# Two-layer encoder trunk: residual and output products kept token by feature, x turned between the layers

## The chip, the cores and the metric

One NeuronCore of one Trainium2 chip runs the whole program in one launch. The metric is the device time of that launch in microseconds, as a median of timed executions. Shapes: 256 tokens, 2048 features, float32 in and out. SBUF and PSUM have 128 partitions, so 256 tokens are two blocks of 128 and 2048 features are sixteen.

## What is computed

Layer 0 has one input projection that feeds attention heads (A) and a gated MLP (B); both halves, side by side, go through one output projection. Layer 1 is a recurrent block with its own input and output projections. Each layer starts with an RMS norm and ends with a residual add, and a last RMS norm closes the program. Cut to what the change touches:

```python
def rms_norm(x, g):
    y = x * lax.rsqrt(jnp.mean(x * x, axis=-1, keepdims=True) + NORM_EPS)
    return y * g

# layer 0: y_a and y_b are (256, 2048) each
x = x + jnp.concatenate([y_a, y_b], axis=-1) @ ab_w_out[0]     # (4096, 2048)
# layer 1: h * silu(z_c) is (256, 2688)
xn = rms_norm(x, c_norm[0])
proj = xn @ c_w_in[0]                                          # (2048, 5376)
...
x = x + (h * jax.nn.silu(z_c)) @ c_w_out[0]                    # (2688, 2048)
return rms_norm(x, final_norm)
```

## The kernel before

Every product is made in three parts from float32 split into a high and a low piece, both of type fp32r: high by high, high by low and low by high. The weights stream from HBM in *chunks*: usually 16 tiles of 128 by 128, as two *units* of 8 tiles (512 KB). For each unit SyncE issues the load into `raw` (L202), ScalarE copies it to `hi` (L220) and VectorE subtracts to get `lo` (L234). `raw`, `hi` and `lo` are rings of 6 buffers, so the splits run up to three chunks ahead of TensorE and the loads up to three more.

`run(emit)` (L268) writes out one chunk: work that was put down with `at(step, fn, phase)` (L253) is called in phases around the two splits and the chunk's matmuls. Phase -1 comes before the splits, 0 to 1.5 between the splits and the matmuls, 2 behind the matmuls. Each engine then runs its own instructions in the order in which they were written; this order is fixed by hand, with no scheduler.

There are two ways to emit a chunk:

- `feat` (L300), *feature by token*: a weight tile is the stationary operand and the activations move. For each tile one matmul of 512 columns takes `hi` against both pieces of x (256 tokens each, L312), and one of 256 columns takes `lo` against the high piece (L316). The output is a block of 128 features by 256 tokens, in two halves that must be added. With `whole=True`, used for the last block of an output product, three matmuls of 256 columns go to one half (L307 to L309).
- `tokn` (L320), *token by feature*: 128 tokens of the activations are stationary and 512 weight columns move. For each row of 128 by 512 weights (four tiles) and each token block three matmuls of 512 columns run (L328 to L330), so 24 for a chunk of 16 tiles. The output is 128 tokens by 512 features, with nothing to add up afterwards. Before the change `tokn` serves v, z_a (`ps_v`, `ps_za`) and the values of B (`ps_vb`).

All three output products go through `feat`: `ob` (the B half of layer 0, `do_ob`, 16 chunks), `oa` (the A half, 16 chunks) and `co` (layer 1, 21 chunks). The residual `res` lies feature by token from the start, since x comes in transposed as `xT`. A finished block is added in two steps (`res_add`, L384).

Between the layers, `x1_add` (L753) forms x's high pieces for layer 1 from the block (times `c_norm`), squares it on ScalarE (L373), and GpSimd adds the squares up in `acc` (L380); `x1_lo` makes the low piece. `norm_at` then sums `acc` over partitions by matmuls with ones (L350), takes the power -0.5 on GpSimd (L356) and spreads it over partitions by matmuls with the identity (L361) into `rb`.

At the end `x2_add` does the same for the last norm and multiplies with `final_norm` on ScalarE (L962). After the last block the sums are formed (L350), raised to -0.5 (L356), spread (L361), and VectorE scales all of `res` in nine pieces, each stored by a DMA from SyncE or ScalarE (L971, L972).

Of the kernel before, what the change touches and what calls it, by code (L numbers as in the profile page):

```python
# [37 lines left out]
for _n, _w in (("g0", KD), ("hn", KD), ("lng", KD), ("lnb", KD), ("g1", KD), ("gf", KD),  # L38
               ("cw0", KC), ("cw1", KC), ("cw2", KC), ("cw3", KC), ("cb", KC),
               ("ba", KC), ("bx", KC), ("lam", KC), ("ident", P)):  # L40
    PRM[_n] = (_at, _w)
    _at += _w
NPRM = _at

# [24 lines left out]
def plan():  # L69
# [23 lines left out]
    def out(kind, rows, wait):  # L93

        cols, late = wait
        order = [(f, k) for f in range(cols) for k in range(late)]
        order += [(f, k) for f in range(cols) for k in range(late, rows)]
        order += [(f, k) for f in range(cols, KD) for k in range(rows)]
        for t in range(0, len(order), 16):
            add(kind, fk=order[t:t + 16], n=len(order[t:t + 16]))  # L100

    heads(0)
    for f in range(KD):
        add("ob", f=f, n=16)
# [4 lines left out]
    out("oa", KD, (4, KD - 4))  # L109
    for j in range(LEAD):  # L110
        add("xb", j=j, n=16)
    for j in range(KC):
        if j + LEAD < KC:
            add("xb", j=j + LEAD, n=16)
# [4 lines left out]
    out("co", KC, (4, KD))  # L119
# [8 lines left out]
def trunk(ctx, tc, xT, prm, rep, wsp, wst, out):  # L128
# [30 lines left out]
    res = cpool.tile([P, KD, S], F32, name="res")  # L159
# [36 lines left out]
    def load(u):  # L196
# [7 lines left out]
        for q in range(a // 4, b // 4):  # L204
            if c == 0 or q == 0 and c < 4:
                ks = slice(q, q + 1) if c == 0 else slice(4 * c, 4 * c + 4)
                SP.dma_start(res[:, ks, :], xT[:, ks, :])
            s = slice((q * 4 - a) * P, (q * 4 - a + 4) * P)
            SP.dma_start(t[:, s], src[:, s])

    def split_x(k):
        A.activation(x.hi[k], res[:, k, :], AF.Copy, scale=par("g0", k))
        V.scalar_tensor_tensor(x.lo[k], res[:, k, :], par("g0", k), x.hi[k].bitcast(F32),
                               op0=ALU.mult, op1=ALU.subtract)
# [105 lines left out]
    def tokn(pss, hi, lo, kq, first, last):  # L320

        for k in range(4):
            s = slice(k * 512, (k + 1) * 512)
            a, b = first and k == 0, last and k == 3
            for t in range(NT):
                xs = slice(t * P, (t + 1) * P)
                xk, xm = x.hi[4 * kq + k][:, xs], x.lo[4 * kq + k][:, xs]
                T.matmul(pss[t], xk, hi[:, s], start=a, stop=False)  # L328
                T.matmul(pss[t], xk, lo[:, s], start=False, stop=False)  # L329
                T.matmul(pss[t], xm, hi[:, s], start=False, stop=b)  # L330
# [13 lines left out]
    def r_sum(more=()):  # L344

        ps = pst.tile([P, 512], F32, tag="t", name="ps_r")
        srcs = [acc, *more]
        for t in range(NT):
            for n, a in enumerate(srcs):
                T.matmul(ps[:, t:t + 1], a[:, t * P:(t + 1) * P], ones[:, 0:1],  # L350
                         start=n == 0, stop=n == len(srcs) - 1)
        return ps

    def r_pow(ps):
        V.tensor_scalar(rt, ps[:, 0:NT], 1.0 / DM, EPS, op0=ALU.mult, op1=ALU.add)
        GP.tensor_tensor(rt, rt, mhalf, op=ALU.pow)  # L356
# [7 lines left out]
    def norm_at(s):  # L364

        box = []
        at(s, lambda: box.append(r_sum()), 2)
        at(s + 1, lambda: r_pow(box[0]))
        at(s + 1, lambda: A.copy(rb, r_spread()[:, :S]), 2)

    def squares(f):
        sq = spool.tile([P, S], F32, tag="sqr", name="sqr")
        A.activation(sq, res[:, f, :], AF.Square)  # L373
        return sq

    def add_squares(f, sq):
        if f == 0:
            GP.tensor_scalar(acc, sq, 1.0, 0.0, op0=ALU.mult, op1=ALU.add)
        else:
            GP.tensor_tensor(acc, acc, sq, op=ALU.add)  # L380

    def res_add(f, ps, whole=False):
        for a in (0, S)[:1 if whole else 2]:
            V.tensor_tensor(res[:, f, :], res[:, f, :], ps[:, a:a + S], op=ALU.add)  # L384
# [10 lines left out]
    def token_chunks(name):  # L395

        pss = [mm_tile(f"ps_{name}_{t}") for t in range(NT)]
        for kq in range(4):
            run(lambda hi, lo: tokn(pss, hi, lo, kq, kq == 0, kq == 3))
        return pss  # L400

# [38 lines left out]
    with tc.tile_pool(name="pb", bufs=2) as pb:  # L440
# [11 lines left out]
        def x_squares(q):  # L452
            A.activation(sq[:, q * 1024:(q + 1) * 1024],
                         res[:, 4 * q:4 * q + 4, :].rearrange("p k s -> p (k s)"), AF.Square)
# [11 lines left out]
        norm_at(5)  # L466
# [142 lines left out]
    with tc.tile_pool(name="pa", bufs=2) as pa:  # L609
# [125 lines left out]
        def do_ob(f):  # L735
            def emit(hi, lo):
                ps = mm_tile(f"ps_ob{f}")
                feat(ps, hi, lo, ALL, y, True, True)
                at(pos[0] + 1, lambda: res_add(f, ps))
            run(emit)  # L740

# [3 lines left out]
        for f in range(KD):  # L745
            do_ob(f)
# [6 lines left out]
        def x1_add(f, ps):  # L753
            res_add(f, ps, f == KD - 1)
            A.activation(x.hi[f], res[:, f, :], AF.Copy, scale=par("g1", f))
            add_squares(f, squares(f))

        def x1_lo(f):
            V.scalar_tensor_tensor(x.lo[f], res[:, f, :], par("g1", f), x.hi[f].bitcast(F32),
                                   op0=ALU.mult, op1=ALU.subtract)  # L760

        def out_product(kind, rows, done):

            cur = {}
            while pos[0] < len(chunks) and chunks[pos[0]]["kind"] == kind:
                def emit(hi, lo):
                    fk = chunks[pos[0]]["fk"]
                    for f in dict.fromkeys(f for f, _ in fk):
                        tiles = [(w, k) for w, (g, k) in enumerate(fk) if g == f]
                        k0, k1 = tiles[0][1], tiles[-1][1]  # L770
                        if k0 == 0:
                            cur[f] = mm_tile(f"ps_{kind}{f}")
                        feat(cur[f], hi, lo, tiles, y, k0 == 0, k1 == rows - 1, f == KD - 1)
                        if k1 == rows - 1:
                            done(f, cur.pop(f), pos[0])
                run(emit)

        def x1_done(f, ps, s):
            if f == KD - 1:
                at(s, lambda: x1_add(f, ps), 2)  # L780
                at(s, lambda: x1_lo(f), 2)
            else:
                at(s + 1, lambda: x1_add(f, ps))
                at(s + 1, lambda: x1_lo(f), 1)
# [5 lines left out]
    with tc.tile_pool(name="pc", bufs=2) as pc:  # L790
# [102 lines left out]
        norm_at(s0)  # L893

        def do_xb(j):
            def emit(hi, lo):
                ps = mm_tile(f"ps_xb{j}")
                feat(ps, hi, lo, ALL, x, True, True)
                s = max(pos[0] + 1, s0 + 2 + (j > 1))
                at(s, lambda: xb_scale(j, ps), -1)  # L900
                at(s, lambda: xb_tap(j), 0.5)
                at(s, lambda: xb_conv(j), 1)
                at(s + 1, lambda: xb_hi(j), 0.5)
                at(s + 1, lambda: xb_lo(j), 1)
            run(emit)

# [34 lines left out]
        for j in range(LEAD):  # L941
            do_xb(j)
        for j in range(KC):
            at(pos[0], lambda j=j: seam(j), 1)
            if j + LEAD < KC:
                do_xb(j + LEAD)
# [6 lines left out]
        last = []  # L953

        def x2_add(f, ps):
            res_add(f, ps, f == KD - 1)
            sq = squares(f)
            if f < KD - 1:
                add_squares(f, sq)
            else:  # L960
                last.append(sq)
            A.activation(res[:, f, :], res[:, f, :], AF.Copy, scale=par("gf", f))  # L962

        out_product("co", KC, lambda f, ps, s: at(min(s + 1, len(chunks) - 1), lambda: x2_add(f, ps),
                                                  2 if s == len(chunks) - 1 else 0))
        r_pow(r_sum(last))
        rbp = r_spread()[:, :S]
        f = 0
        for q, w in enumerate((1, 1, 2, 2, 2, 2, 2, 2, 2)):
            fs = slice(f, f + w)  # L970
            V.tensor_tensor(res[:, fs, :], res[:, fs, :], rbp.unsqueeze(1).broadcast_to([P, w, S]), op=ALU.mult)  # L971
            (SP, A)[q % 2].dma_start(out[:, fs, :], res[:, fs, :])  # L972
            f += w


def pack(np, i):
# [9 lines left out]
    for c in chunks:  # L986
# [12 lines left out]
        elif kind == "ob":  # L999
            src = rows(wo0, KD, KD, P * c["f"], P)  # L1000
        elif kind in ("xb", "zc"):
            src = rows(w1, 0, KD, (kind == "zc") * CW + P * c["j"], P)
        elif kind in ("oa", "co"):
            src = np.concatenate([rows(wo0 if kind == "oa" else wo1, k, 1, P * f, P) for f, k in c["fk"]], axis=1)
# [26 lines left out]
    put("gf", i["final_norm"])  # L1031
# [9 lines left out]
    rep = np.concatenate([i["ab_sgu_b"][0].reshape(-1), i["ab_lambda"][0].reshape(-1)])  # L1041
# [22 lines left out]
```

## Time and profile before

| | us |
|---|---|
| median of 3 runs (lowest to highest) | 1248.69 (1248.47 to 1249.19) |
| the profiled execution's own time | 1249.09 |
| its span, first to last instruction | 1247.3 |
| TensorE matmul busy | 1234.3 (99%) |
| VectorE busy | 868.0 (70%) |
| ScalarE busy | 680.6 (55%) |
| GpSimd busy | 62.8 (5%) |
| HBM traffic over the span | 185 GB/s |

The span is the profiled execution's time less 1.79 us outside the first and last instruction. Busy times are shares of the span. A matmul's printed duration overlaps the next one's, so rates of TensorE are read from the distance of starts, not from durations. The chain of waits follows what ended last back to the start.

### The profile page before, as it was taken

The page shows a single profiled execution, that of the slowest core. Times are in us where ns is not written, and L with a number is a line of the kernel's source. Part 1 is how long each engine was busy: PE and PEld are TensorE (multiplying, and loading weights), DVE is VectorE, ACT ScalarE, POOL GpSimd, SP SyncE. Part 2 cuts the span into 40 slices and gives each one's busy share as a digit, 9 for nine tenths or more (in the row PEclk, how much of TensorE's full clock was granted, in tenths as well). Part 3 has the DMA queues.
Part 4 walks back from the last instruction along what each step waited for, and adds up shares of the span by engine and source line. Part 5 has one row for each costly group of instructions (what it writes and reads, how often), then busy time and mean ns, then how long its engine had stood idle before and what let it go on. Part 6 is the DMA issues. An engine that isn't in the chain of part 4 may idle for free.

```text
span 1247.3 us, 18370 instructions
## 1 busy us (share of the span) xinstructions
PE 1234.3 (99%) x6903; PEld 1080.2 (87%) x6903; DVE 868.0 (70%) x1359; ACT 680.6 (55%) x1093; POOL 62.8 (5%) x96
## 2 busy tenths in 40 slices
PE   9999999999999999999999999999999999999996
PEld 7888888888888888888888888888889889988885
DVE  6847777776566646646746746767899999988553
ACT  7544454444454344544444545545788887886541
POOL 1100000000000000000000000110000000001111
PEclk9999999999999999999999999999999999999998
DMA  9854555555645654555555555564655666657541
GB/s 331 283 181 168 184 184 182 184 179 190 204 148 182 199 194 167 189 180 169 186 174 173 183 178 171 189 199 154 198 196 201 220 194 201 199 179 237 190 135 68
DMA packets 69400, 234.57 MB, mean 188 GB/s; under 512 B 8000, under 2 KB 8896, under 8 KB 69312
## 3 DMA queue, kind: packets, MB, share of 16 engines
q1 hardware_dynamic: 66240, 227.84, 54.8%
q0 software_dynamic: 1920, 3.15, 1.0%
q10 hardware_dynamic: 1152, 2.42, 0.6%
q8 instruction: 54, 0.88, 0.3%
q14 instruction: 34, 0.28, 0.1%
HBM read 228.13 MB, written 2.10 MB: 185 GB/s over the span
## 4 chain that ended last, share of the span: by engine, by line
PE 97%; issue 1%; DVE 1%; DMA 1%; SPq 0%; ACT 0%; POOLq 0%; POOL 0%; DVEq 0%; ACTq 0%
PE ps_xb L312 6%; PE ps_zc L312 6%; PE ps_co L312 6%; PE ps_zb L312 5%; PE ps_k L312 5%; PE ps_ob L312 5%; PE ps_q L312 5%; PE ps_u L312 5%; PE ps_oa L312 4%; PE ps_zc L316 3%; PE ps_xb L316 3%; PE ps_co L316 3%; PE ps_k L316 2%; PE ps_ob L316 2%; PE ps_u L316 2%; PE ps_q L316 2%
## 5 line engine op out<-in xcount | busy, mean ns | idle before, releaser
L234 DVE TENSOR_TENSOR lo<-raw,hi 128x1024 fp32r<-128x1024 f32 (+2 forms) x423 | 503.4, 1205 | 185.4 <-ACT hi L220 180.2
L220 ACT CAST hi<-raw 128x1024 fp32r<-128x1024 f32 (+2 forms) x423 | 427.2, 1037 | 246.4 <-PE ps_za L330 50.0
L312 PE MATMUL ps_xb<-x,hi 128*128 128x512 f32 x336 | 83.8, 392 | 0.0
L312 PE MATMUL ps_zc<-x,hi 128*128 128x512 f32 x336 | 83.6, 391 | 0.0
L312 PE MATMUL ps_co<-y,hi 128*128 128x512 f32 x315 | 77.8, 391 | 0.0
L312 PEld LDWEIGHTS ps_zc<-x,hi 128*128 128x128 f32 x336 | 61.8, 188 | 11.8
L312 PEld LDWEIGHTS ps_xb<-x,hi 128*128 128x128 f32 x336 | 61.8, 188 | 11.2
L312 PEld LDWEIGHTS ps_co<-y,hi 128*128 128x128 f32 x315 | 56.9, 189 | 10.3
L312 PE MATMUL ps_zb<-x,hi 128*128 128x512 f32 x256 | 65.0, 396 | 0.0
L312 PE MATMUL ps_q<-x,hi 128*128 128x512 f32 x256 | 63.7, 393 | 0.0
L312 PE MATMUL ps_u<-x,hi 128*128 128x512 f32 x256 | 63.7, 391 | 0.0
L312 PE MATMUL ps_k<-x,hi 128*128 128x512 f32 x256 | 63.4, 393 | 0.0
L312 PE MATMUL ps_ob<-y,hi 128*128 128x512 f32 x256 | 62.8, 394 | 0.0
L312 PE MATMUL ps_oa<-y,hi 128*128 128x512 f32 x240 | 59.0, 392 | 0.5 <-DVE res L384 0.5
L312 PEld LDWEIGHTS ps_u<-x,hi 128*128 128x128 f32 x256 | 47.0, 188 | 9.1
L312 PEld LDWEIGHTS ps_q<-x,hi 128*128 128x128 f32 x256 | 47.1, 188 | 9.0
L312 PEld LDWEIGHTS ps_ob<-y,hi 128*128 128x128 f32 x256 | 47.1, 188 | 9.0
L312 PEld LDWEIGHTS ps_k<-x,hi 128*128 128x128 f32 x256 | 47.1, 188 | 8.9
L312 PEld LDWEIGHTS ps_zb<-x,hi 128*128 128x128 f32 x256 | 47.1, 189 | 8.5
L312 PEld LDWEIGHTS ps_oa<-y,hi 128*128 128x128 f32 x240 | 43.7, 188 | 8.9 <-PE ps_oa L312 0.9
L328 PE MATMUL ps_vb<-hi,x 128*128 128x512 f32 x128 | 51.1, 399 | 0.2 <-ACT hi L226 0.2
L329 PE MATMUL ps_vb<-lo,x 128*128 128x512 f32 x128 | 50.3, 393 | 0.7 <-DVE lo L227 0.7
(296 smaller groups left out, 2302.5 us busy)
## 6 DMA issues: line engine op xcount, KB each, us to landing
raw<-in_wst SPq DMA_DIRECT2D x402, 512.0 KB, 3.9
raw<-in_wst SPq DMA_DIRECT2D x30, 256.0 KB, 6.0
raw<-in_wst SPq DMA_DIRECT2D x15, 384.0 KB, 3.3
seam<-xcp POOLq DMA_DIRECT2D x9, 192.0 KB, 3.1
res<-in_xT SPq DMA_DIRECT2D x3, 512.0 KB, 6.9
out_x<-res SPq DMA_DIRECT2D x4, 256.0 KB, 2.3
seam<-xcp POOLq DMA_DIRECT2D x6, 128.0 KB, 2.3
out_x<-res ACTq DMA_DIRECT2D x3, 256.0 KB, 2.4
```

The source lines that it names most:

```text
L220: A.copy(hi[:, :(b - a) * P], raw[u][:, :(b - a) * P])
L234: V.tensor_sub(lo[:, :n], raw[u][:, :n], hi[:, :n].bitcast(F32))
L312: wide = lambda i: T.matmul(ps, hi[:, col(tiles[i][0])], m.both[tiles[i][1]], start=first and i == 0, stop=last and i == n - 1)
L316: T.matmul(ps[:, :S], lo[:, col(w)], m.hi[k], start=False, stop=False)
L328: T.matmul(pss[t], xk, hi[:, s], start=a, stop=False)
L329: T.matmul(pss[t], xk, lo[:, s], start=False, stop=False)
```

## The change

The residual `res` becomes token by feature: 128 tokens by 2048 features for each of two token blocks. It takes the room of the feature-major copy of x, which only the first chunks read; a second copy of x, `xt`, 2 MB in token layout, is loaded into that room at step 24 by two DMAs of ScalarE's queue.

The three output products use `tokn`, in four column blocks `cb` of 512 features. A chunk is four rows of 128 by 512 weights; in `co` (21 rows) the last chunk of a column block has five, so `co` has 20 chunks instead of 21. The residual add is one 512-column step for each token block. The squares are summed along the features by ScalarE's accumulating output (`ssq`), so GpSimd's additions and the matmuls with ones go in layer 1 and at the end.

Layer 1 still wants x feature by token. So after each column block of `oa`, eight TensorE transposes (`x1_turn`) bring it to PSUM, and ScalarE and VectorE make the high and low pieces from there (`x1_parts`). To leave time for the last column block, the first two chunks of `xb` take rows 0 to 11 of the first two feature blocks first and rows 12 to 15 last (`early`).

At the end `final_norm`, copied over 128 partitions, is loaded at step `s1 + 8` by eight DMAs of ScalarE's queue (1 MB) and multiplied in for column blocks 0 to 2 by VectorE while `co` runs (`gf_mult`). The last chunk does the first token block's matmuls, then the second's (`apart`); each token block is then normed, scaled and stored by itself (`finish`), with all eight stores on SyncE.

```diff
-    def out(kind, rows, wait):
-        cols, late = wait
-        order = [(f, k) for f in range(cols) for k in range(late)]
...
+    def out(kind, rows):
+
+        for cb in range(4):
+            for k in range(0, rows - 3, 4):
+                nk = rows - k if rows - k < 8 else 4
+                add(kind, cb=cb, k0=k, nk=nk, n=4 * nk)
...
+    early = [(j, k) for j in range(2) for k in range(12)] + [(j, k) for j in range(2) for k in range(12, KD)]
+    xb = lambda jk: add("xb", jk=jk, n=16)
+    xb(early[:16])
+    xb(early[16:])
...
-    def tokn(pss, hi, lo, kq, first, last):
+    def tokn(pss, hi, lo, m, k0, nk, first, last, apart=False):
+
+
+        for k, t in [(k, t) for t in range(NT) for k in range(nk)] if apart else \
+                [(k, t) for k in range(nk) for t in range(NT)]:
             s = slice(k * 512, (k + 1) * 512)
...
+            T.matmul(pss[t], mh, hi[:, s], start=a, stop=False)
+            T.matmul(pss[t], mh, lo[:, s], start=False, stop=False)
+            T.matmul(pss[t], ml, hi[:, s], start=False, stop=b)
...
+    def q_sum(ts=slice(0, NT)):
+
+        V.tensor_reduce(rt[:, ts], ssq[:, ts, :], axis=AX.X, op=ALU.add)
+        return rt[:, ts]
...
+    def res_add(cb, pss, t):
+        f = slice(cb * 512, (cb + 1) * 512)
+        V.tensor_tensor(res[:, t, f], res[:, t, f], pss[t], op=ALU.add)
+
+    def squares(cb, t):
+        A.activation(sqs, res[:, t, cb * 512:(cb + 1) * 512], AF.Square, accum_out=ssq[:, t, cb:cb + 1])
...
+        at(24, lambda: [A.dma_start(res[:, t, :], xt[:, t, :]) for t in range(NT)], 1)
...
+        def x1_turn(cb):
+            pts = []
+            for h in range(2):
+                ps = pst.tile([P, 512], F32, tag="to"[h], name=f"ps_x{cb}_{h}")
+                pts.append(ps)
+                for e in range(2):
+                    for t in range(NT):
+                        f = (4 * cb + 2 * h + e) * P
+                        T.transpose(ps[:, e * S + t * P:e * S + (t + 1) * P], res[:, t, f:f + P], ident)
+            return pts
+
+        def x1_parts(cb, pts):
+            for a in range(4):
+                k, v = 4 * cb + a, pts[a // 2][:, a % 2 * S:a % 2 * S + S]
+                A.activation(x.hi[k], v, AF.Copy, scale=par("g1", k))
+                V.scalar_tensor_tensor(x.lo[k], v, par("g1", k), x.hi[k].bitcast(F32),
+                                       op0=ALU.mult, op1=ALU.subtract)
+
+        def x1_done(cb, pss, s):
+            box = []
+            for t in range(NT):
+                at(s + 1, lambda t=t: res_add(cb, pss, t), -1)
+                at(s + 1, lambda t=t: squares(cb, t))
+            at(s + 1, lambda: box.append(x1_turn(cb)), 2)
+            at(s + 2, lambda: x1_parts(cb, box[0]), -1)
...
-        norm_at(s0)
...
+        at(s0, lambda: r_pow(q_sum()), 1.5)
+        spread_at(s0 + 1)
...
+        at(s1 + 8, gf_load)
...
+            if s < len(chunks) - 1:
+                at(s + 1, lambda: [res_add(cb, pss, t) for t in range(NT)])
+                at(s + 1, lambda: [squares(cb, t) for t in range(NT)], 1)
+                at(max(s + 2, s1 + 10), lambda: gf_mult(cb), 1)
+                return
+            for t in range(NT):
+                at(s, lambda t=t: (res_add(cb, pss, t), squares(cb, t), finish(t)), 2)
+
+        def finish(t):
+
+
+            ts = slice(t, t + 1)
+            r_pow(q_sum(ts), ts)
+            sc = rt[:, ts]
+            for n, (a, b) in enumerate(((0, 512), (1024, 1536), (512, 1024), (1536, 2048))):
+                r = res[:, t, a:b]
+                if n % 2 == 0:
+                    A.activation(r, r, AF.Copy, scale=sc)
+                elif b < DM:
+                    V.tensor_scalar_mul(r, r, sc)
+                else:
+                    for c in range(a, b, S):
+                        r = res[:, t, c:c + S]
+                        V.scalar_tensor_tensor(r, r, sc, gf[c // S], op0=ALU.mult, op1=ALU.mult)
+                SP.dma_start(out[:, t, a:b], res[:, t, a:b])
```

How this moves instructions is shown at three places. First, TensorE at the start of the B half's output product. Before (one chunk, one feature block):

```order
L312 MATMUL ps_ob_3239<-y,hi_3148 128x512
L316 MATMUL ps_ob_3239<-y,lo_3149 128x256 x8
L316 MATMUL ps_ob_3239<-y,lo_3153 128x256 x8
L312 MATMUL ps_ob_3239<-y,hi_3148 128x512 x7
L312 MATMUL ps_ob_3239<-y,hi_3152 128x512 x8
```

Now, the first quarter of a chunk (`ps_ob_0` and `ps_ob_1` are the two token blocks):

```order
L337 MATMUL ps_ob_0_3229<-hi_3152,y 128x512
L338 MATMUL ps_ob_0_3229<-lo_3153,y 128x512
L339 MATMUL ps_ob_0_3229<-hi_3152,y 128x512
L337 MATMUL ps_ob_1_3230<-hi_3152,y 128x512
L338 MATMUL ps_ob_1_3230<-lo_3153,y 128x512
L339 MATMUL ps_ob_1_3230<-hi_3152,y 128x512
```

Sixteen matmuls of 512 columns and sixteen of 256 have become 24 of 512.

Second, TensorE where layer 0 ends and `xb`, the first input product of layer 1, begins. Before:

```order
L309 MATMUL ps_oa_7467<-y,lo_7349 128x256
L312 MATMUL ps_xb_7541<-x,hi_7396 128x512
L316 MATMUL ps_xb_7541<-x,lo_7397 128x256 x8
L316 MATMUL ps_xb_7541<-x,lo_7401 128x256 x8
L312 MATMUL ps_xb_7541<-x,hi_7396 128x512 x7
L312 MATMUL ps_xb_7541<-x,hi_7400 128x512 x8
L350 MATMUL ps_r<-ones,acc 128x1 x2
L312 MATMUL ps_xb_7591<-x,hi_7448 128x512
```

Now, from the end of the first `xb` chunk to the end of the second (`ps_xb_7195` is feature block 0, `ps_xb_7220` block 1, `ps_x` the transposes):

```order
L320 MATMUL ps_xb_7220<-x,hi_7101 128x512
L324 MATMUL ps_xb_7220<-x,lo_7102 128x256 x4
L320 MATMUL ps_xb_7220<-x,hi_7101 128x512 x3
L772 MATMUL ps_x_0_7229<-pt,res 128x128 x4
L772 MATMUL ps_x_1_7234<-pt,res 128x128 x4
L320 MATMUL ps_xb_7220<-x,hi_7133 128x512
L324 MATMUL ps_xb_7220<-x,lo_7134 128x256 x8
L320 MATMUL ps_xb_7220<-x,hi_7133 128x512 x7
L320 MATMUL ps_xb_7195<-x,hi_7137 128x512
L324 MATMUL ps_xb_7195<-x,lo_7138 128x256 x4
L320 MATMUL ps_xb_7195<-x,hi_7137 128x512 x3
```

The transposes of the last column block stand where the matmuls with ones stood, and eight tiles of rows 4 to 11 stand between them and the first matmul that reads the new rows 12 to 15 (block 0, `hi_7137`).

Third, VectorE at the end of the program. Before:

```order
L384 TENSOR_TENSOR res<-res,ps_co_11710 128x256 x2
L384 TENSOR_TENSOR res<-res,ps_co_11759 128x256
L355 TENSOR_SCALAR rt<-ps_r 128x2
L971 TENSOR_TENSOR res<-res,ps_rb 128x256 x2
L971 TENSOR_TENSOR res<-res,ps_rb 128x512 x7
```

Now, the first token block and the add of the second:

```order
L382 TENSOR_TENSOR res<-res,ps_co_0_11089 128x512
L362 TENSOR_REDUCE rt<-ssq 128x1
L366 TENSOR_SCALAR rt<-rt 128x1
L1008 TENSOR_SCALAR res<-res,rt 128x512
L1012 SCALAR_TENSOR_TENSOR res<-res,rt,qgf__10808 128x256
L1012 SCALAR_TENSOR_TENSOR res<-res,rt,qgf__10810 128x256
L382 TENSOR_TENSOR res<-res,ps_co_1_11090 128x512
```

The scaling of one token block stands ahead of the residual add of the other, and the nine scalings that followed everything are gone.

## Rows read from the trace of the kernel before

**Rows 1.** The page: span, traffic in 40 equal slices, chain that ended last

```profile
span 1247.3 us, 18370 instructions
...
GB/s 331 283 181 168 184 184 182 184 179 190 204 148 182 199 194 167 189 180 169 186 174 173 183 178 171 189 199 154 198 196 201 220 194 201 199 179 237 190 135 68
...
PE 97%; issue 1%; DVE 1%; DMA 1%; SPq 0%; ACT 0%; POOLq 0%; POOL 0%; DVEq 0%; ACTq 0%
```

**Rows 2.** Timeline (start, duration in us), TensorE, last z_a matmuls, first of `oa`

```profile
744.76 0.39 PE L330 MATMUL ps_za<-hi,x 128*128 128x512 f32 x1
...
751.11 0.39 PE L312 MATMUL ps_oa<-y,hi 128*128 128x512 f32 x1
```

**Rows 3.** Timeline, TensorE, starts of two chunks of `oa`, nine chunks apart

```profile
780.84 2.08 PE L316 MATMUL ps_oa<-y,lo 128*128 128x256 f32 x16
...
830.94 2.08 PE L316 MATMUL ps_oa<-y,lo 128*128 128x256 f32 x16
```

**Rows 4.** Timeline, eight transposes amid `oa`, their readers, and an idle stretch

```profile
762.27 1.03 PE L711 MATMUL ps_y<-pt,on 128*128 128x128 f32 x8
...
763.06 0.48 PE L312 MATMUL ps_oa<-y,hi 128*128 128x512 f32 x1
763.38 0.64 PE L316 MATMUL ps_oa<-y,lo 128*128 128x256 f32 x4
763.42 1.56 ACT L717 ACTIVATE y<-ps_y,hnp 128x256 fp32r<-128x256 f32 x4
...
764.69 1.66 DVE L723 SCALAR_TENSOR_TENSOR y<-ps_y,hnp,y 128x256 fp32r<-128x256 f32 x4
...
774.97 0.47 PE L312 MATMUL ps_oa<-y,hi 128*128 128x512 f32 x1 [0.47 <-DVE res L384]
```

**Rows 5.** Timeline, TensorE, start of layer 1

```profile
842.03 0.40 PE L312 MATMUL ps_xb<-x,hi 128*128 128x512 f32 x1
...
847.64 0.50 PE L350 MATMUL ps_r<-ones,acc 128*128 128x1 f32 x4
848.00 0.49 PE L312 MATMUL ps_xb<-x,hi 128*128 128x512 f32 x1
```

**Rows 6.** Timeline, TensorE, first matmul of `co`

```profile
1117.21 0.39 PE L312 MATMUL ps_co<-y,hi 128*128 128x512 f32 x1
```

**Rows 7.** `co` stretch: length, busy PE, PEld, DVE, ACT, POOL; clock, DMA share, GB/s

```profile
1117.20:1234.50 117.30, 117.30 (x695) 104.29 (x694) 68.28 (x92) 61.42 (x86) 16.54 (x15) 1.00 0.48 157
```

**Rows 8.** Timeline of the end, from the last product's end

```profile
1234.49 0.28 PE L350 MATMUL ps_r<-ones,acc 128*128 128x1 f32 x2
1234.69 0.42 DVE L384 TENSOR_TENSOR res<-res,ps_co 128x256 f32<-128x256 f32 x1 [6.68 <-PE ps_co L309]
1235.20 0.42 ACT L373 ACTIVATE sqr<-res 128x256 f32<-128x256 f32 x1 [6.14 <-DVE res L384]
...
1236.54 0.16 DVE L355 TENSOR_SCALAR rt<-ps_r 128x2 f32<-128x2 f32 x1 [1.43 <-PE ps_r L350]
1236.78 0.72 POOL L356 TENSOR_TENSOR rt<-rt,mhalf 128x2 f32<-128x2 f32 x1 [7.37 <-DVE rt L355]
1237.55 1.03 PE L361 MATMUL ps_rb<-pt,rt 128*128 128x128 f32 x4 [1.05 <-POOL rt L356]
1238.62 4.94 DVE L971 TENSOR_TENSOR res<-res,ps_rb 128x256 f32<-128x256 f32 x9 [1.93 <-PE ps_rb L361]
```

**Rows 9.** Groups by line and shape: count | busy us, mean ns of one

```profile
L700 DVE SCALAR_TENSOR_TENSOR tz<-tz,ps_za 128x512 f32<-128x512 f32 x8 | 5.4, 680 | 0.0
...
L499 ACT ACTIVATE vx<-ps_vb,rt 128x512 f32<-128x512 f32 x8 | 5.0, 681 | 0.0
...
L677 ACT ACTIVATION_READ_ACCUMULATOR sq<-ps_o 128x1 f32 x16 | 3.1, 195 | 0.0
```

**Rows 10.** By tile `out_x`: issues, ns min/median/max, first and last start

```profile
L972 SPq DMA_DIRECT2D out_x<-res x5: 332/333/348, 1239.1 to 1243.6; - x5
```

**Rows 11.** By tile `ps_vb`, the program's first product: ns min/median/max, first and last start

```profile
L328 PE MATMUL ps_vb<-hi,x x128: 387/389/799, 5.9 to 97.0; 128*128 128x512 f32 x128
```

More of the change, by code (lines that the diff above doesn't have):

```diff
@@ L43 @@
 NPRM = _at
+GF = (G + 4) * P
 def gate_rows(j):
@@ L91, in za @@
             add("za", p=p, kq=kq, n=16)
-    def out(kind, rows, wait):
-        cols, late = wait
-        order = [(f, k) for f in range(cols) for k in range(late)]
[L97 to L100, printed above, removed]
+    def out(kind, rows):
[3 more added lines that the diff above has]
+                add(kind, cb=cb, k0=k, nk=nk, n=4 * nk)
     heads(0)
-    for f in range(KD):
-        add("ob", f=f, n=16)
+    out("ob", KD)
     za(0)
@@ L118, in plan @@
     add("zc", j=KC - 1, n=16)
-    out("co", KC, (4, KD))
+    out("co", KC)
     off = 0
@@ L318, in feat @@
             wide(i)
-    def tokn(pss, hi, lo, kq, first, last):
-        for k in range(4):
+    def tokn(pss, hi, lo, m, k0, nk, first, last, apart=False):
+        for k, t in [(k, t) for t in range(NT) for k in range(nk)] if apart else \
+                [(k, t) for k in range(nk) for t in range(NT)]:
             s = slice(k * 512, (k + 1) * 512)
[L324 to L330, printed above, removed]
+            a, b = first and k == 0, last and k == nk - 1
+            ts = slice(t * P, (t + 1) * P)
+            mh, ml = m.hi[k0 + k][:, ts], m.lo[k0 + k][:, ts]
+            T.matmul(pss[t], mh, hi[:, s], start=a, stop=False)
+            T.matmul(pss[t], mh, lo[:, s], start=False, stop=False)
+            T.matmul(pss[t], ml, hi[:, s], start=False, stop=b)
     ALL = [(k, k) for k in range(KD)]
@@ L341, in mm_tile, with r_sum, r_pow @@
         return pmm.tile([P, 512], F32, tag="mm", name=name)
-    def r_sum(more=()):
+    def r_sum():
         ps = pst.tile([P, 512], F32, tag="t", name="ps_r")
-        srcs = [acc, *more]
         for t in range(NT):
[L349 to L356, printed above, removed]
+            T.matmul(ps[:, t:t + 1], acc[:, t * P:(t + 1) * P], ones[:, 0:1], start=True, stop=True)
+        return ps[:, 0:NT]
+    def q_sum(ts=slice(0, NT)):
+        V.tensor_reduce(rt[:, ts], ssq[:, ts, :], axis=AX.X, op=ALU.add)
+        return rt[:, ts]
+    def r_pow(ps, ts=slice(0, NT)):
+        V.tensor_scalar(rt[:, ts], ps, 1.0 / DM, EPS, op0=ALU.mult, op1=ALU.add)
+        GP.tensor_tensor(rt[:, ts], rt[:, ts], mhalf[:, ts], op=ALU.pow)
     def r_spread():
@@ L362, in r_spread, with spread_at @@
         return ps
[L364 to L384, printed above, removed]
+    def spread_at(s):
+        at(s, lambda: A.copy(rb, r_spread()[:, :S]), 2)
+    sqs = spool.tile([P, 512], F32, tag="sqr", name="sqr", bufs=1)
+    def res_add(cb, pss, t):
[3 more added lines that the diff above has]
+        A.activation(sqs, res[:, t, cb * 512:(cb + 1) * 512], AF.Square, accum_out=ssq[:, t, cb:cb + 1])
     state = {}
@@ L398, in token_chunks, with out_product, emit @@
         for kq in range(4):
-            run(lambda hi, lo: tokn(pss, hi, lo, kq, kq == 0, kq == 3))
+            run(lambda hi, lo: tokn(pss, hi, lo, x, 4 * kq, 4, kq == 0, kq == 3))
         return pss
+    def out_product(kind, rows, done):
+        while pos[0] < len(chunks) and chunks[pos[0]]["kind"] == kind:
+            c = chunks[pos[0]]
+            if c["k0"] == 0:
+                pss = [mm_tile(f"ps_{kind}{c['cb']}_{t}") for t in range(NT)]
+            end = c["k0"] + c["nk"] == rows
+            def emit(hi, lo):
+                tokn(pss, hi, lo, y, c["k0"], c["nk"], c["k0"] == 0, end, pos[0] == len(chunks) - 1)
+                if end:
+                    done(c["cb"], pss, pos[0])
+            run(emit)
     def v_evac(pss, v):
@@ L733, in do_za @@
             at(s + 2, lambda: y_lo(p), 1)
[L735 to L740, printed above, removed]
         at(pos[0], lam_dots, 2)
         at(pos[0] + 8, softplus)
-        for f in range(KD):
-            do_ob(f)
+        out_product("ob", KD, lambda cb, pss, s: at(s + 1, lambda: [res_add(cb, pss, t) for t in range(NT)]))
         do_za(0)
@@ L750, in trunk @@
             do_za(p)
[L753 to L776, printed above, removed]
@@ L950, in trunk @@
         do_z(KC - 1)
[L953 to L973, printed above, removed]
+        gf, s1 = [], pos[0]
+        def gf_load():
+            for a in range(DM // S):
+                gf.append(tl("th" if a < 4 else "q", f"gf{a}_", 4))
+                A.dma_start(gf[a], rep[:, GF + a * S:GF + (a + 1) * S])
```

101 lines of the change are left out of this document (60 added, 41 removed).

## The prediction

> **What bounds the kernel now.** I read the page first: TensorE is the chain that ended last for 97% of the span [rows 1]. So a stage is worth what its stream of matmuls takes from start to start; the other engines count only where TensorE waits for them, and in the tail behind the last product. Then I read the timeline of TensorE at the places that the change touches, and at last the timeline of the tail.
>
> The rates come from starts. The last z_a matmuls are the form that all output products will have: 28 starts from 744.76 to 751.11 give 6.35 / 28 = 0.2268 us for one of 512 columns [rows 2], so 24 x 0.2268 = 5.443 us for a chunk of 16 tiles. The feature-by-token form takes (830.94 - 780.84) / 9 = 5.567 us a chunk [rows 3]. The columns are equal (24 x 512 against 16 x 512 + 16 x 256); the difference, 0.124 us, is eight instructions fewer. Stages: `oa` runs from 751.11 to 842.03, 90.92 us [rows 2, 5]; `co` from 1117.21 to 1234.49, 117.28 us [rows 6, 8]; the tail from there to the end of the span at 1247.3, 12.81 us [rows 1, 8].
>
> **The change part by part.**
>
> *B half.* The product is sixteen chunks beside the same attention work: 16 x 0.124 = **-1.98 us**.
>
> *A half.* 384 matmuls x 0.2268 = 87.09 us. In this stage stand the eight transposes of z_a's gating, as before, and eight more after each of column blocks 0 to 2. One such group costs 763.06 - 762.27 = 0.79 us, and the first wide matmul behind it takes 763.38 - 763.06 = 0.32 instead of 0.23, so 0.88 [rows 4]. 87.09 + 4 x 0.88 = 90.61 against 90.92: **-0.31 us**. Gone with the old order are the idle 0.47 us [rows 4] and the three-part last block; the transposes eat nearly all of it.
>
> *Start of layer 1.* The fourth group of transposes adds 0.88; the four matmuls with ones go, 848.00 - 847.64 = 0.36 [rows 5] and again about 0.1 of restart: **+0.42 us**. Does TensorE wait there? Let T be the start of the first `xb` chunk. The residual adds begin when the last block is done and take 2 x 0.68 us (512 columns, [rows 9]), so the transposes, which come behind the chunk at T + 5.6, find their data. They end at T + 6.4. Four high pieces on ScalarE took 1.56 us and four low ones on VectorE, which ended 766.35 - 763.42 = 2.93 us after the first began, 1.66 [rows 4]; so rows 12 to 15 are complete at about T + 9.5. The new order puts eight tiles of old rows in front, 8 x 5.567 / 16 = 2.8 us [rows 3], so row 12 is wanted at T + 9.2 and row 15's low piece only five matmuls and more later, near T + 10.4. Row 12's pieces are the first of the four. So no wait, but with about 1 us to spare.
>
> *Layer 1's product.* 84 rows of weights x 6 x 0.2268 = 114.31 against 117.28: **-2.97 us**. The twelve multiplications with `final_norm` for three column blocks lie on VectorE, which is busy 68 of the 117 us here [rows 7]; at 0.42 us each (256 columns, the residual add of [rows 8]) that is 5 us in 49 free. If that cover were gone they would lengthen the tail.
>
> *The tail.* Call E the end of the stream (1234.49 before). Before, 12.81 us: add, squares, sums by matmul, power, spread, nine scalings, last store [rows 8]. Now token block 0 ends 15 matmuls before E, at E - 3.40. Add from E - 3.20 (the lag of 0.20 is that of [rows 8]) to E - 2.52; squares 0.68 and the accumulator's read 0.20 [rows 9] with 0.09 for the hop, to E - 1.55; a reduction of four numbers and the small scaling at 0.16 each with hops, to E - 1.05; power 0.72 [rows 8], to E - 0.25. VectorE then scales: 0.68 for 512 columns at the most, two steps of 0.415 (a quarter of 1.66, [rows 4]), to E + 1.3. **A new wait** stands here: behind the instruction that waits for GpSimd's power, VectorE has queued these scalings and then the add of token block 1, which could start at E + 0.20 and starts at E + 1.3. ScalarE, GpSimd and SyncE all wait for that add. From there: add to 1.99, squares and read to 2.95, two small steps to 3.45, power to 4.25, ScalarE's two scalings of 0.68 to 5.66, VectorE's to 5.81. Stores on SyncE take 0.33 us of issue each [rows 10], so the last is issued at about E + 6.0. Before, the last store was issued at 1243.6 [rows 10] and the span ended 3.7 us later; I take the same, E + 9.73. **-3.08 us**. Bounds: without the new wait E + 8.6 (-4.2); with both powers at twice 0.72 and a lag of 0.3 more, E + 11.5 (-1.3).
>
> *Loads.* The second copy of x is 2 MB in a stretch that moves 168 to 184 GB/s, where the first slice shows 331 [rows 1]; with some 150 GB/s free it takes about 14 us beside the stream. The loads run three chunks (16 us) ahead of the splits and these three ahead of TensorE, so nothing. If that cover failed, the most is 2 MB at 331 GB/s, 6.3 us. `final_norm` is half of that, where 157 GB/s move [rows 7]; its eight issues hold ScalarE for 8 x 0.33 = 2.7 us [rows 10] with 56 of 117 us free: nothing.
>
> Sum: -1.98 - 0.31 + 0.42 - 2.97 - 3.08 = -7.92. On the profiled execution's 1249.09 that is 1241.17; it lies 0.40 above the median 1248.69, so the median becomes **1240.8 us**.
>
> The rows show a fixed part in each matmul: a tile pair takes 5.567 / 16 = 0.348 us, so 256 columns take 0.348 - 0.2268 = 0.121, and 2 x 0.121 - 0.2268 leaves about 15 ns that don't go with columns [rows 2, 3]. That part is what the change saves. The Trainium skill, "TensorE: Matmul & The Clock Gate", section "Back-to-back issue gap", gives columns / 2.4 plus 2.5 ns for an isolated gap; this trace has 226.8 ns where that has 215.8. By the page's figures the saving, an estimate, would be 1.3 ns a tile instead of 7.7, and the whole sum about -2.5.
>
> **The rivals.**
>
> *The fixed part is not saved* (4%). The saving hangs on output products running at z_a's step of 0.2268. If their step is 0.348 / 1.5 = 0.2319 us, each pair of tiles costs what it cost, and 53 chunks x 0.124 = 6.6 us go from the sum: 1247.4. Against it: z_a, beside the same loads and splits, keeps 0.2268 over all 28 starts. The Trainium skill's formula named above (the page on TensorE) points this way.
>
> *Slower* (5%). The same place, further: if the matmuls wait a little for operands, as in the program's first product, where 381 steps from 5.9 to 97.0 give 0.2391 us [rows 11], the three products' 1272 matmuls cost 1272 x 0.0123 = 15.6 us more: 1256.4. It is slower than before by over 0.2% (2.5 us) from 0.2268 + (7.9 + 2.5) / 1272 = 0.235 us. For it: the output products now write 512-column adds, squares and a second use of VectorE beside the splits. Against it: that first product starts with empty rings and the first loads; z_a shows no such loss.
>
> *A wait at the start of layer 1* (10%). There is 1 us to spare. If ScalarE or VectorE reach the last pieces late, by the work of one chunk's splits, TensorE stands 2 to 4 us: 1242.8 to 1244.8. For it: the reads of PSUM pieces come just behind the transposes; against it: the splits of that chunk are written behind the pieces.
>
> *The tail gains nothing* (7%). If the token blocks don't overlap (the first block's chain takes the time of the second), 12.8 us stay: 1243.9.
>
> *More than forecast* (6%). The tail without the new wait, and transposes that hide: 1237.5 to 1239.
>
> **How the numbers follow.** My forecast, 1239 to 1242.6 by the tail's bounds and some tenths on the stream, has 68%. The range of 1238.0 to 1244.8 takes in the wait, the tail without gain and half of the last case; the two on the fixed part and slower and bits of the others, under 2 in 10, stay out. 0.2%, 2.5 us, is about what a measurement of this kernel can tell from no change. Faster by more than that (below 1246.2): 68 + 10 + 7 + 6 = 91%. Within: the fixed part, 4%. Slower: 5%.
>
> **What would show it.** In the profile after: 24 starts of `ps_ob`, `ps_oa` and `ps_co` in 5.44 us; `oa` 90.6 us long and `co` 114.3; eight transposes in 0.8 us, four times; no idle time of TensorE in the first two `xb` chunks; VectorE's add of token block 1 1.1 us later than its matmuls allow; a tail of 9.7 us. I am wrong if the step is longer than 0.2268, if TensorE waits for x's pieces, or if GpSimd's power or the stores take longer for two half-size rounds than for one.

## The result, and the profile after

| | before | after |
|---|---|---|
| median of 4 runs each (lowest to highest), us | 1248.61 (1248.47 to 1249.19) | 1240.82 (1240.51 to 1241.34) |
| ratio to before, 95% interval | | 0.9937 (0.9924 to 0.9949) |
| the profiled execution's own time, us | 1249.09 | 1240.98 |
| its span, us | 1247.3 | 1239.2 |

The change gains 7.8 us, 0.6%. Five more runs of it on another occasion gave 1240.83 (1240.34 to 1241.16).

The page of the kernel after: span, busy times of the engines, traffic in 40 equal slices, the chain that ended last, and two groups of DMA issues (KB each, us to landing).

```profile
span 1239.2 us, 17358 instructions
...
PE 1228.1 (99%) x6458; PEld 1056.9 (85%) x6458; DVE 844.1 (68%) x1304; ACT 673.6 (54%) x1083; POOL 34.9 (3%) x66
...
GB/s 329 278 188 170 238 202 173 186 187 176 213 156 187 193 196 172 187 170 174 184 174 167 191 174 179 170 189 172 202 192 198 215 205 203 207 179 228 223 178 68
...
PE 98%; DMA 1%; DVE 0%; SPq 0%; issue 0%; ACT 0%; ACTq 0%; POOLq 0%; POOL 0%; DVEq 0%
...
res<-in_xt ACTq DMA_DIRECT2D x2, 1024.0 KB, 7.2
out_x<-res SPq DMA_DIRECT2D x8, 256.0 KB, 2.4
```

TensorE is still the chain that ended last. GpSimd's additions are gone, and its busy time falls from 62.8 to 34.9 us. The load of the second copy of x shows in the fifth slice, 238 GB/s against 184 before [rows 1].

TensorE's timeline of the kernel after (start and duration in us) at the borders of the stages, in the order of the program:

```profile
349.54 0.39 PE L337 MATMUL ps_ob<-hi,y 128*128 128x512 f32 x1
...
443.03 0.39 PE L337 MATMUL ps_za<-hi,x 128*128 128x512 f32 x1
...
749.71 0.39 PE L337 MATMUL ps_oa<-hi,y 128*128 128x512 f32 x1
...
840.43 0.39 PE L320 MATMUL ps_xb<-x,hi 128*128 128x512 f32 x1
...
1116.07 0.39 PE L337 MATMUL ps_co<-hi,y 128*128 128x512 f32 x1
...
1230.08 0.39 PE L339 MATMUL ps_co<-hi,y 128*128 128x512 f32 x1
```

The last matmul starts at 1230.08, so the stream ends at 1230.08 + 0.227 = 1230.31 and `co` lasts 114.24 us: 504 matmuls at 0.2267, the step of z_a [rows 2]. The borders of `ob` in TensorE's timeline of the kernel before:

```profile
349.24 0.39 PE L312 MATMUL ps_ob<-y,hi 128*128 128x512 f32 x1
...
444.45 0.39 PE L328 MATMUL ps_za<-hi,x 128*128 128x512 f32 x1
```

Stage by stage, with the same borders before (the others in [rows 2, 5, 6, 8]):

| stretch | before | after | difference | forecast |
|---|---|---|---|---|
| start to `ob` | 349.24 | 349.54 | +0.30 | 0 |
| `ob`, with attention between | 95.21 | 93.49 | -1.72 | -1.98 |
| to `oa` | 306.66 | 306.68 | +0.02 | 0 |
| `oa` | 90.92 | 90.72 | -0.20 | -0.31 |
| layer 1 up to `co` | 275.18 | 275.64 | +0.46 | +0.42 |
| `co` | 117.28 | 114.24 | -3.04 | -2.97 |
| tail | 12.81 | 8.89 | -3.92 | -3.08 |
| span | 1247.3 | 1239.2 | -8.10 | -7.92 |

The first line is no effect of the change: in nine profiles of this kernel and its variants `ob` starts between 348.8 and 350.1 us. They come apart in the first 15 us, where TensorE waits for the first pieces; why these come at different times was not traced.

The tail in the timeline of the kernel after; what is in brackets is the idle time before and its releaser:

```profile
1227.11 0.69 DVE L382 TENSOR_TENSOR res<-res,ps_co 128x512 f32<-128x512 f32 x1 [10.21 <-PE ps_co L339]
1227.89 0.63 ACT L385 ACTIVATE sqr<-res 128x512 f32<-128x512 f32 x1 [11.72 <-DVE res L382]
1228.43 0.19 ACT L385 ACTIVATION_READ_ACCUMULATOR sqr<-res 128x1 f32 x1
...
1229.08 0.57 POOL L367 TENSOR_TENSOR rt<-rt,mhalf 128x1 f32<-128x1 f32 x1 [152.62 <-DVE rt L366]
1229.68 1.34 ACT L1006 ACTIVATE res<-res,rt 128x512 f32<-128x512 f32 x2 [1.07 <-POOL rt L367]
1229.69 0.48 DVE L1008 TENSOR_SCALAR res<-res,rt 128x512 f32<-128x512 f32 x1 [0.69 <-POOL rt L367]
...
1230.48 0.48 DVE L1012 SCALAR_TENSOR_TENSOR res<-res,rt,qgf__10810 128x256 f32<-128x256 f32 x1
1230.88 0.68 DVE L382 TENSOR_TENSOR res<-res,ps_co 128x512 f32<-128x512 f32 x1
...
1233.42 1.33 ACT L1006 ACTIVATE res<-res,rt 128x512 f32<-128x512 f32 x2 [1.04 <-POOL rt L367]
...
1234.22 0.48 DVE L1012 SCALAR_TENSOR_TENSOR res<-res,rt,qgf__10810 128x256 f32<-128x256 f32 x1
```

SyncE's own timeline of the same kernel, the last four stores, which it issues in line:

```profile
1234.17 1.80 SPq L1013 DMA_DIRECT2D out_x<-res  x4
```

Token block 0 is normed and half scaled when TensorE stops at 1230.31. The add of block 1 stands behind block 0's scalings on VectorE without a gap and starts at 1230.88. One chain of add, squares, power and scalings follows; the last four stores are issued over 1.80 us.

Where layer 1 begins, the pieces of the last column block and their reader, in the timeline of the kernel after:

```profile
846.01 1.03 PE L772 MATMUL ps_x<-pt,res 128*128 128x128 f32 x8
846.65 0.47 ACT L778 ACTIVATE x<-ps_x,pt 128x256 fp32r<-128x256 f32 x1 [3.59 <-PE ps_x L772]
846.80 0.48 PE L320 MATMUL ps_xb<-x,hi 128*128 128x512 f32 x1
...
847.15 0.48 DVE L779 SCALAR_TENSOR_TENSOR x<-ps_x,pt,x 128x256 fp32r<-128x256 f32 x1 [3.29 <-ACT x L778]
...
849.60 0.48 DVE L779 SCALAR_TENSOR_TENSOR x<-ps_x,pt,x 128x256 fp32r<-128x256 f32 x1 [0.54 <-ACT x L778]
...
849.92 0.64 PE L324 MATMUL ps_xb<-x,lo 128*128 128x256 f32 x4
850.39 1.09 PE L320 MATMUL ps_xb<-x,hi 128*128 128x512 f32 x4
```

Row 12's low piece is there at 847.63 and its first reader starts one step of 0.23 before 849.92, 2.1 us later. The last low piece is there at 850.08; row 15's matmul is the third of the row at 850.39, near 850.85: 0.8 us to spare. TensorE shows no idle time here.

### The profile page after: what moved, and what is told of

The parts are those of the page before. It is cut to its first block, busy times and chain, and to the rows that moved or that the text cites. A ratio compares the mean times of both kernels' runs of the same rounds, so it can differ in the third digit from the quotient of the medians.

```text
span 1239.2 us, 17358 instructions
## 1 busy us (share of the span) xinstructions
PE 1228.1 (99%) x6458; PEld 1056.9 (85%) x6458; DVE 844.1 (68%) x1304; ACT 673.6 (54%) x1083; POOL 34.9 (3%) x66
## 4 chain that ended last, share of the span: by engine, by line
PE 98%; DMA 1%; DVE 0%; SPq 0%; issue 0%; ACT 0%; ACTq 0%; POOLq 0%; POOL 0%; DVEq 0%
PE ps_xb L320 6%; PE ps_zc L320 6%; PE ps_zb L320 5%; PE ps_k L320 5%; PE ps_q L320 5%; PE ps_u L320 5%; PE ps_zc L324 3%; PE ps_xb L324 3%; PE ps_co L339 3%; PE ps_co L337 3%; PE ps_co L338 3%; PE ps_q L324 2%; PE ps_u L324 2%; PE ps_k L324 2%; PE ps_zb L324 2%; PE ps_v L337 2%
## 5 line engine op out<-in xcount | busy, mean ns | idle before, releaser
L337 PE MATMUL ps_co<-hi,y 128*128 128x512 f32 x168 | 65.4, 389 | 0.0
L338 PE MATMUL ps_co<-lo,y 128*128 128x512 f32 x168 | 65.4, 389 | 0.0
L339 PE MATMUL ps_co<-hi,y 128*128 128x512 f32 x168 | 65.4, 389 | 0.0
L337 PE MATMUL ps_v<-hi,x 128*128 128x512 f32 x128 | 50.7, 396 | 0.0
L337 PE MATMUL ps_ob<-hi,y 128*128 128x512 f32 x128 | 50.6, 395 | 0.0
L337 PE MATMUL ps_za<-hi,x 128*128 128x512 f32 x128 | 50.4, 394 | 0.0
```

Of the source, the lines that this page charges most:

```text
L337: T.matmul(pss[t], mh, hi[:, s], start=a, stop=False)
L338: T.matmul(pss[t], mh, lo[:, s], start=False, stop=False)
L339: T.matmul(pss[t], ml, hi[:, s], start=False, stop=b)
```

## The experiments

The theory: the products gain by issuing fewer matmuls of the same columns; the transposes stand on TensorE's path; the reordered first two `xb` chunks hide the pieces of the last column block; and the tail is shorter because one token block is finished under the other's matmuls.

The first four kernels below ran on an occasion on which the kernel before took 1249.08 us (ten runs), 0.5 above its 1248.61 in the result, and the changed kernel did not run beside them. So the distance of their medians from 1240.82 is good to about half a microsecond. The traces say more: from one profile to the next, a stage that an edit leaves alone keeps its length within 0.02 us, from `ob` to `co`.

**Fewer instructions or something else?** In the B half's product every matmul is cut in two, save the first and the last of each accumulation.

```diff
-            T.matmul(pss[t], mh, hi[:, s], start=a, stop=False)
-            T.matmul(pss[t], mh, lo[:, s], start=False, stop=False)
-            T.matmul(pss[t], ml, hi[:, s], start=False, stop=b)
+            for i, (l, r) in enumerate(((mh, hi), (mh, lo), (ml, hi))):
+                on, off = a and i == 0, b and i == 2
+                v = 512 if on or off else w
+                for c in range(0, 512, v):
+                    T.matmul(pss[t][:, c:c + v], l, r[:, k * 512 + c:k * 512 + c + v], start=on, stop=off)
...
+                     w=256 if kind == "ob" else 512)
```

> The changed kernel, but in the product of the B half (ob) each matmul of 512 columns becomes two of 256, save the first and the last of each accumulation: 384 instructions become 752, with the same columns. Theory (each matmul has a fixed part beside its columns, and the change gains by issuing fewer): before the change 48 matmuls of 256 columns at the end of oa took 841.91 + 0.12 - 836.28 = 5.75 us, 0.1198 each, against 0.2268 for 512, so two halves cost 0.013 more than one whole; 368 more instructions give +4.7 us on the changed kernel's 1240.8, about 1245.5. Rival (TensorE's time goes with the columns alone and the gain came from elsewhere): +0. Second rival (weight loads of 188 ns set the step): 736 x (0.188 - 0.1134) = +55 us.

Measured: 1245.1 us (1244.8 to 1246.0), 4.3 more than the changed kernel, ratio to before 0.9968 (0.9957 to 0.998). TensorE's timeline of this kernel, first matmul of `ob` and first behind it:

```profile
350.14 0.39 PE L341 MATMUL ps_ob<-hi,y 128*128 128x512 f32 x1
...
448.06 0.40 PE L341 MATMUL ps_za<-hi,x 128*128 128x512 f32 x1
```

The stage takes 97.92 us where the changed kernel's takes 93.49: +4.43 us for 368 more instructions, 12.0 ns each. The columns are the same, so columns alone don't set TensorE's time, and the length of the weight loads (+55 us) doesn't either. The theory's 12.8 ns from rows of 256 and 512 columns holds to a tenth. Each added matmul brings a weight load of its own, so the 12.0 ns belong to the pair; which of the two they belong to isn't shown.

**Are the transposes on the path?** This kernel leaves the turn out and reads the residual as it lies, so layer 1 computes on other numbers.

```diff
-            at(s + 1, lambda: box.append(x1_turn(cb)), 2)
-            at(s + 2, lambda: x1_parts(cb, box[0]), -1)
+            at(s + 2, lambda: x1_parts(cb), -1)
...
-                k, v = 4 * cb + a, pts[a // 2][:, a % 2 * S:a % 2 * S + S]
+                k = 4 * cb + a
+                v = res[:, a // 2, cb * 512 + a % 2 * S:cb * 512 + a % 2 * S + S]
```

> The changed kernel without the 32 transposes between the layers: x's pieces are made from residual columns as they lie, so the values of layer 1 are not the reference's. Theory (the transposes stand on TensorE's path, 0.88 us for each group of eight with the restart): -3.5 us, about 1237.3; oa at 88.1 instead of 90.7 us. Rival (they hide beside other work, or the pieces set the time anyway): 0 to -1.

Measured: 1237.3 us (1237.2 to 1237.7), 3.5 less than the changed kernel. Start of `oa` and of `xb` in its timeline of TensorE:

```profile
749.41 0.39 PE L337 MATMUL ps_oa<-hi,y 128*128 128x512 f32 x1
...
837.37 0.39 PE L320 MATMUL ps_xb<-x,hi 128*128 128x512 f32 x1
```

`oa` lasts 87.96 us instead of 90.72: 2.76 for three groups of eight, 0.92 each. They stand on the path in full. The fourth group stands in the second `xb` chunk: the spread's matmul, which follows that chunk, starts 11.17 us behind the first `xb` matmul (837.37 to 848.54) instead of 12.06 (840.43 to 852.49), 0.89 less. Later in layer 1 this kernel loses 0.3 us of that again, at the first matmul that reads `seam` (1004.83).

**Does the reordering at the start of layer 1 hide anything?**

```diff
-    xb(early[16:])
+    xb([(0, k) for k in range(12, KD)] + [(1, k) for k in range(4, KD)])
```

> The changed kernel, but the second xb chunk takes rows 12 to 15 of feature block 0 first instead of after eight tiles of old rows. Theory (the pieces of the last column block come 0.8 to 3.3 us behind the transposes and the eight tiles hide them): TensorE waits at that place, in all some 2 us, 1.8 to 2.5 longer than the changed kernel. Rival (the reordering hides nothing since the pieces are ready): 0.

Measured: 1242.8 us (1242.5 to 1243.6), 2.0 more than the changed kernel. For whom TensorE waited in this kernel (total us, times, longest); its other waits lie at the program's start, as in the changed kernel:

```profile
PE ps_xb L324 <- ACT x L778: 0.7, 1, 0.7
PE ps_xb L320 <- DVE x L779: 0.6, 1, 0.6
```

TensorE waits for the first low piece and for the last high piece. The printed waits give 1.3 us; they are counted from modelled ends, which overlap the next start by some 0.16 to 0.26 at each wait. By starts the first two chunks with the transposes between them are longer by 2.2 us: the spread's matmul begins 14.30 us behind the first `xb` matmul (839.72 to 854.02) instead of 12.06 (840.43 to 852.49). The wait that the forecast named as a rival is real, and the eight tiles of old rows are what hides it.

**Is it the overlap that shortens the tail?** The last chunk alternates the token blocks again.

```diff
-                tokn(pss, hi, lo, y, c["k0"], c["nk"], c["k0"] == 0, end, pos[0] == len(chunks) - 1)
+                tokn(pss, hi, lo, y, c["k0"], c["nk"], c["k0"] == 0, end)
```

> The changed kernel, but the last chunk alternates the token blocks as all others do, so that token block 0 ends 0.68 us before the end of the stream and not 3.40. Theory (the tail is shorter because block 0's norm, scaling and stores run under block 1's matmuls): +2.7 us less what the wait for VectorE already costs, 2.3 to 2.7 longer than the changed kernel, tail of 11.2 to 11.6 instead of 8.9. Rival (the tail got shorter because sums by matmul and the spread are gone and half-size steps are quicker, not by the overlap): 0 to +0.5.

Measured: 1243.9 us (1243.1 to 1244.4), 3.1 more than the changed kernel. From its timeline, the last matmul and the two adds:

```profile
1229.29 0.69 DVE L382 TENSOR_TENSOR res<-res,ps_co 128x512 f32<-128x512 f32 x1 [12.93 <-PE ps_co L339]
...
1229.54 0.39 PE L339 MATMUL ps_co<-hi,y 128*128 128x512 f32 x1
...
1233.05 0.68 DVE L382 TENSOR_TENSOR res<-res,ps_co 128x512 f32<-128x512 f32 x1
```

The stream ends at 1229.54 + 0.227 = 1229.77 and the span at 1241.4, a tail of 11.6 us against 8.9: +2.7, the upper end of what was expected. (The median rose by 3.1, which lies above that range by less than the half microsecond to which such a distance is good.) The first add comes 0.48 us before the end of the stream instead of 3.20, and the whole chain moves with it; VectorE's second add still stands behind the first block's scalings, 3.76 us after the first add as in the changed kernel (1227.11 to 1230.88). Without the overlap the tail keeps 12.8 - 11.6 = 1.2 of its 3.9 us.

**What is left in the tail.** Two edits, alone and together, beside the changed kernel. In the first, the add of block 1 moves ahead of the last of block 0's scalings:

```diff
-            for t in range(NT):
-                at(s, lambda t=t: (res_add(cb, pss, t), squares(cb, t), finish(t)), 2)
+            at(s, lambda: (res_add(cb, pss, 0), squares(cb, 0), finish(0, lambda: res_add(cb, pss, 1)),
+                           squares(cb, 1), finish(1)), 2)
...
+                        if between and c > a:
+                            between()
```

In the second, the stores follow the order in which their data is ready, and one of the last four goes to ScalarE's queue:

```diff
-                SP.dma_start(out[:, t, a:b], res[:, t, a:b])
+            for n, a in ((1, 1024), (0, 0), (2, 512), (3, 1536)):
+                (A if n == 2 and t else SP).dma_start(out[:, t, a:a + 512], res[:, t, a:a + 512])
```

> The changed kernel as it is, beside the next three on one chip: 1240.8 within 0.5.

> The changed kernel, but VectorE's residual add of token block 1 stands ahead of the last scaling of token block 0 instead of behind it. Theory (the add waits behind the scalings: it started 0.57 us behind the end of the stream, where the add of block 0 started 0.20 behind its matmuls): the add comes 0.3 to 0.4 us earlier and all of block 1's chain with it, -0.3 us. Rival (the end is set by SyncE's issue of the last four stores, which follow each other at 0.42 to 0.5 us): their first starts 0.3 earlier too, unless the scalings of ScalarE and VectorE delay it; 0 to -0.1 then.

> The changed kernel, but the stores of a token block are issued in the order in which VectorE and ScalarE finish them, and the third of the last four goes to ScalarE's queue. In the changed kernel SyncE starts the last four at 1234.17, 1234.59, 1235.07 and about 1235.6, and the data of the last is ready at 1234.75. Theory (the issues in line cost the last store 0.8 us): the last starts at about 1234.85, -0.7 us. Rival (the drain of the stores, not their issue, sets the end): 0.

> Both edits together. If each holds by itself: -1.0 us, about 1239.8, faster than the changed kernel; if only the stores count, -0.7.

| kernel | median of 5, us (lowest to highest) | stream's end | span's end | tail |
|---|---|---|---|---|
| changed, again | 1240.83 (1240.34 to 1241.16) | 1229.68 | 1238.6 | 8.9 |
| add early | 1240.99 (1240.48 to 1241.75) | 1230.79 | 1239.3 | 8.5 |
| stores | 1240.35 (1240.16 to 1240.82) | 1230.35 | 1239.0 | 8.7 |
| both | 1240.38 (1240.04 to 1241.33) | 1230.11 | 1238.4 | 8.3 |

By the traces, the early add shortens the tail by 0.4 us and both edits by 0.6, where 0.3 and 1.0 were expected. In five profiles of kernels that leave the tail as it is (the changed kernel twice, the first three variants) it lasts 8.9 us within 0.05, so by the traces these differences are real. By the times, none of it is shown: the medians lie up to 0.5 us below the changed kernel's, but the runs overlap, and the streams end up to 1.1 us apart from one profile to the next, more than the edits are worth. So no version here beats the changed kernel beyond doubt.

The stores missed their 0.7 us. In the timeline of ScalarE, in the kernel of that edit alone, its store:

```profile
1234.84 0.38 ACTq L1014 DMA_DIRECT2D out_x<-res  x1
```

In the same kernel's timeline of SyncE, the three of the last four that it still issues, and in a later window the last of them:

```profile
1233.98 1.30 SPq L1014 DMA_DIRECT2D out_x<-res  x3
...
1234.88 0.40 SPq L1014 DMA_DIRECT2D out_x<-res  x1
```

The last issue is at 4.5 us behind the stream's end instead of 5.2 (1235.55 in the changed kernel), as expected. But the span ends 4.2 us behind it, not 3.65: the longest time from issue to landing rose from 2.7 to 3.2 us. The issue saved 0.7 us and the landing gave back 0.5. The end goes with the first of the last four stores and not with the last: from its start to the end of the span it is 5.0 us in the changed kernel (1234.17), with this edit (1233.98), with the early add (1234.28) and with both (1233.38). The edit starts this first store 3.63 us behind the stream's end instead of 3.86, and the 0.2 us gained are no more than that. So the traces side with the rival: the landing of the stores sets the end, and not the issue of the last one. That they get into each other's way there is inferred from these numbers.

## Why the prediction was right, point by point

*The bound.* The forecast took TensorE's starts as the measure of each stage, and the stages came out within 0.3 us of it, save the tail.

*The rate.* All three products run at z_a's step: 114.24 us for `co` where 114.31 stood. That most of the saving lies in a fixed part of each matmul (with its weight load) is shown by cutting them: at 12.0 ns an instruction, eight fewer are 0.096 of the 0.124 us a chunk. The rest was not taken apart; in the kernel before, three wide matmuls in most chunks of `ob` step at 0.233 to 0.236 instead of 0.227, some 0.02 us a chunk. The Trainium skill, "TensorE: Matmul & The Clock Gate", section "Back-to-back issue gap", has 2.5 ns beside the columns, for an isolated gap; this trace differs and decides, for this type of operand and this stream. With the step as forecast, both rivals on the step (fixed part not saved, slower) are out: there is no row of TensorE waiting for an operand in the three output products. The price of the rival *Slower* was read too high besides: among the 381 steps of [rows 11] stand twelve matmuls of other work, 2.6 us together, and some 2 us of waits and restarts before 14 us; the median step of the first product, too, is 0.227.

*The B half.* -1.72 instead of -1.98. With the chunks at the step, what lies between them takes 93.49 - 16 x 5.443 = 6.40 us where it took 95.21 - 16 x 5.567 = 6.14. The term took this part as unchanged, and it is 0.26 longer. By starts, the attention's own matmuls take 5.46 us in place of 5.37, 0.1 of it in one longer gap between two transposes of `ps_t` (0.38 us from the one at 374.39 to the next, where it had been 0.29). The other 0.17 lie in the product's own matmuls, of which some behind each piece of attention step at 0.235; why isn't shown.

*The A half and the start of layer 1.* -0.20 and +0.46 against -0.31 and +0.42; a group of transposes costs 0.92 in `oa`, not 0.88. Leaving all four out gave back, by the medians, the 3.5 us that the sum had for them. The forecast had about 1 us to spare, from all pieces ready at T + 9.5 to row 15's reader at T + 10.4. (T is the start of the first `xb` chunk.) Measured, they were ready at T + 9.65 and the reader came at T + 10.42, 0.8 to spare, and 2.1 at row 12. The pieces took 3.4 us (846.65 to 850.08) where [rows 4] had 2.9: ScalarE and VectorE wait for each other between them, about 0.55 us each time, which those rows don't show.

*The loads.* Free, as forecast. The stretch of 31 us around them, after and before (length, busy PE, PEld, DVE, ACT, POOL; clock, DMA share, GB/s):

```profile
125.00:156.00 31.00, 31.00 (x184) 27.48 (x183) 22.16 (x37) 13.91 (x24) 0.00 (x0) 1.00 0.71 247
...
125.00:156.00 31.00, 31.00 (x184) 27.51 (x184) 22.25 (x37) 14.21 (x24) 0.00 (x0) 1.00 0.55 184
```

The traffic rises from 184 to 247 GB/s and the weights land in 4.1 us instead of 3.3 (medians of this stretch; the longest in 8.8 instead of 4.7), but TensorE is busy all of it.

*The tail* is the term that was mis-sized: -3.92 instead of -3.08. The power of one column took 0.57 us, not the 0.72 of two columns; the squares with the accumulator's read took 0.73 us, since the read begins before the squares' printed end, not 0.88; VectorE's scalings took 1.27 us, not 1.51. So block 1's add started 0.57 us behind the stream and not 1.3, and with the same savings in block 1's own chain its data were ready 4.4 us behind the stream (1234.75) and not 5.8. The stores gave back 0.5 of these 1.4: the span ended 4.4 us behind the data, where the sum had 3.9. The new wait was there, but worth 0.4 us where 1.1 was forecast: moving the add in front of one scaling shortened the tail by that. The overlap itself was right: without it, 2.7 us come back.

*The total* came out at the forecast, 1240.82 against 1240.8, with a tail 0.8 better against 0.3 lost at the start, 0.3 in the B half and 0.15 around the transposes. Save for the tail its parts are right to about 0.3 us; that the errors cancel to hundredths is luck.

## What to carry to other kernels

Where one engine is busy all the time, count its instructions and not only its columns: the same product in 24 wide matmuls instead of 16 wide and 16 narrow ones was 2% quicker, and a few transposes gave half of that back. Work behind the last product is paid in full, so let the last product finish one part of the output early and carry that part to its store under the rest. When a layout change puts a conversion between two stages, give the next stage something to do that doesn't need it: here eight tiles were worth 2 us.

## What the runs showed of the hardware that was not expected

A 512-column operation of ScalarE with an accumulating output and the read of that output took 0.73 us together, less than the 0.63 and 0.19 of its two rows. Stores issued in line on SyncE started 0.42, 0.48 and about 0.5 us apart (1234.17, 1234.59, 1235.07, then about 1235.55), though one issue had taken 0.33 us before [rows 10]; putting one of them on a second queue, in another order, brought the last issue forward by 0.7 us and the end by 0.2, no more than the first of the four had moved. From the first of these four stores to the end of the span it was 5.0 us in each of four kernels.
